# Order of the accumulating transfers of a head, and which weight loads the block copies follow, in a one-core hybrid block

## The chip, the core and the metric

The kernel runs on one core of one Trainium2 chip. The metric is the device time of one execution in microseconds (us); the time before is the median of three runs. A part of the reference's work is done on TensorE (called PE in the profile), with VectorE (DVE) and ScalarE (ACT) beside it; GpSimd (POOL) and SyncE (SP) issue the transfers, which sixteen DMA engines carry out.

## The reference

For 512 tokens of 1024 features the reference computes one layer: a projection with a wide weight matrix `w_in`, two mixers (a gated delta rule A with 8 heads, and a chunked retention B with 4 heads), their gated sum, and a feed-forward block. What the change touches is the part of `w_in` that makes the values and the gates of the four heads of mixer B:

```python
proj = xn @ w_in
qa, ka, va, za, beta_logit, a_dt, qb, kb, vb, gb, gate_a, gate_b = _split_cols(proj, IN_SIZES)
...
ob = chunk_retention(qb, kb, vb)
ob = rmsnorm(ob, norm_b.reshape(B_HEADS, B_DV)) * jax.nn.silu(gb.reshape(b, s, B_HEADS, B_DV))
yb = ob.reshape(b, s, B_V) @ w_br_b
```

For each head, `vb` and `gb` are 512 columns each.

## The kernel before, in words

**Products.** Every float32 product is made of three matmuls (`mm3`, L82 to L84) on a value that is split in a high and a low part. A weight is fetched 512 KB at a time by `weights` (L86): SP issues the load into one of the `raw` buffers (two in the first pool; a second pool adds two from head 0 of mixer B on), ACT casts it to its high part `whi` (L109), DVE subtracts to get the low part `wlo` (L110). `whi` and `wlo` have three buffers each. In most stages one such load feeds 24 matmuls of 128x512. Products land in four PSUM buffers `mm`, which ACT or DVE empty (for instance `acc`, L441 on ACT in the first partial product of a branch, L443 on DVE in the later ones). Engines run their instructions strictly in the order in which a scheduler wrote them at build time, so an ACT cast that waits for its load also holds up whatever ACT has behind it, and a DVE subtraction whatever DVE has behind it.

**Block sums.** The values and the gates of a head of mixer B are one product of four blocks by seven multiplications instead of eight (`values_and_gates`, L761). Four sums of weight blocks are needed for it; `BlockSums` (L116) makes them in DRAM without any compute engine. Each of the four sums `t[0]` to `t[3]` of a head has 1 MB and is handled in two halves of 512 KB (`k` is 0 or 2):

- A *copy* (L128) brings a first block from `w_in` to `t[i]`, DRAM to DRAM, on SP's queue. There are 32 of them. A list, `trickle`, holds them in the order head 0, 1, 2, 3; `weights` counts its loads from 0 (the counter `loads`) and issues one copy behind each load whose number is odd and at least 13 (L96 to L99).
- An *add* (`add`, L130) is an accumulating transfer that POOL issues: `t[2] += w12`, `t[1] += t[2]`, `t[3] += t[1]`, `t[0] += w12`, each in two halves. An add that reads another's result waits for it to land; POOL stands still while it waits. The eight adds of a head are issued behind one marked POOL instruction: head 0 and head 1 in stage A, behind the last transfer of `double_blocks` or the mask of `values_queries` (L719 to L721), heads 2 and 3 in mixer B behind the load of a decay table (L845 to L848).

The sums of head h are read back as weights (`raw<-sums`, L144) only when head h of mixer B is computed, from 592 us on for head 0.

**Stages.** Mixer A (up to about 540 us) has keys, values and queries, an inverse on DVE (L510 to L519) with small transfers on POOL's queue, four steps of a recurrence, gates, and the partial products of branch A (`ya_partial`, L436); then the four heads of mixer B, the output product, and the feed-forward block. The scheduler interleaves neighbouring stages.

**Order of work.** SP's queue carries loads and copies in one order; POOL's queue carries the adds, small memsets for the convolution (L397) and the small transfers of the inverse.

Of the kernel before, what the change touches and what calls it, by code (L numbers as in the profile page):

```python
# [15 lines left out]
ALU = mybir.AluOpType  # L16
# [44 lines left out]
def hybrid_block_kernel(ctx: ExitStack, tc: tile.TileContext, a: dict, out: bass.AP):  # L61
    nc = tc.nc
# [9 lines left out]
    trickle = []  # L72
# [13 lines left out]
    def weights(src, k0, nk, c0, ncols, keep=None):  # L86

        n = nk * ncols
        i = next(loads)
        pool, tag = raw_pools[i % len(raw_pools)]  # L90
        raw = pool.tile([P, 1024], F32, tag=tag, name="raw", bufs=2)
        load = nc.sync.dma_start(
            raw[:, :n].rearrange("p (k c) -> p k c", k=nk),
            src[k0 * P : (k0 + nk) * P, c0 : c0 + ncols].rearrange("(k p) c -> p k c", p=P),
        )
        if i >= 13 and i % 2 and trickle:  # L96
            sums, part, k = trickle.pop(0)
            with tc.issue_after(load.ins):
                sums.copy(part, k)  # L99
        return split_weights(raw, n, nk, keep, 200 if i >= 6 else 0)  # L100

    def split_weights(raw, n, nk, keep=None, ahead=200):
        if keep is None:
            hi = ring.tile([P, 1024], F32R, tag="whi", name="whi")
            lo = ring.tile([P, 1024], F32R, tag="wlo", name="wlo")
        else:
            hi, lo = keep
        with tc.high_priority(ahead):
            nc.scalar.copy(hi[:, :n], raw[:, :n])  # L109
            nc.vector.tensor_tensor(lo[:, :n], raw[:, :n], hi[:, :n], ALU.subtract)  # L110
        return (
            hi[:, :n].rearrange("p (k c) -> p k c", k=nk),
            lo[:, :n].rearrange("p (k c) -> p k c", k=nk),
        )

    class BlockSums:  # L116
# [12 lines left out]

        def add(self):  # L130

            for i in (2, 1, 3, 0):
                src = (self.w12, self.t[2], self.w12, self.t[1])[i]
                for k in range(0, 4, 2):
                    nc.gpsimd.dma_start(self.t[i][:, k : k + 2, :], src[:, k : k + 2, :], accum_op=ALU.add)

        def weights(self, i, ks):
            return block_weights(self.t[i - 1][:, 2 * ks : 2 * ks + 2, :])
# [8 lines left out]
    def feature_major(src, xs, c0, ncols, kts, krow0=0):  # L147

        nf = ncols // P
        pss = [psm.tile([P, xs[0].shape[2]], F32, tag="mm", name="mm") for _ in range(nf)]  # L150
        step = 1024 // ncols
        for k0 in range(0, kts, step):
            wh, wl = weights(src, krow0 + k0, step, c0, ncols)
            for f in range(nf):
                fs = slice(f * P, (f + 1) * P)
                for kk in range(step):
                    kt = k0 + kk
                    mm3(
                        pss[f],
                        (wh[:, kk, fs], wl[:, kk, fs]),  # L160
                        (xs[0][:, kt, :], xs[1][:, kt, :]),
                        kt == 0,
                        kt == kts - 1,
                    )
        return pss

    def token_major(src, lhs, c0, kts, krow0=0):

        pss = [psm.tile([P, T], F32, tag="mm", name="mm") for _ in range(4)]
        for k0 in range(0, kts, 2):  # L170
            wh, wl = weights(src, krow0 + k0, 2, c0, 512)
            for t in range(4):
                tt = slice(t * P, (t + 1) * P)
                for kk in range(2):
                    kt = k0 + kk
                    mm3(
                        pss[t],
                        [x[:, tt] for x in lhs(kt)],
                        (wh[:, kk, :], wl[:, kk, :]),
                        kt == 0,  # L180
                        kt == kts - 1,
                    )
        return pss
# [71 lines left out]
    with tc.tile_pool(name="xp", bufs=2) as xp:  # L255
# [30 lines left out]
        for pair in range(2):  # L286
            v = xp.tile([P, 2], F32, tag="xv", name="xv")
            for i in range(2):
                junk = xp.tile([P, D], BF16, tag="junk", name="junk")
                nc.scalar.activation(junk, xts[2 * pair + i], AF.Square, accum_out=v[:, i : i + 1])  # L290
            nc.vector.tensor_scalar(v, v, 1.0 / D, EPS, ALU.mult, ALU.add)
            y = root(v)
            rx += [y[:, i : i + 1] for i in range(2)]
            if pair == 0:
                wh, wl = weights(w_in, 0, 8, OFF_BA, P)
# [862 lines left out]
```

## Time and profile before

| | us |
|---|---|
| median of 3 runs | 1410.09 |
| lowest and highest | 1409.16, 1411.61 |
| the profiled execution, its own time | 1413.15 |
| its span, first to last instruction | 1411.4 |
| PE busy | 1378.8 |
| DVE busy | 868.5 |
| ACT busy | 613.5 |

The mean granted clock of TensorE was 0.991. In the profile a row of a timeline gives start, duration, engine, source line, what is written and read, and in brackets how long the engine had been idle and what ended the wait. A `q` behind an engine's name means its queue: an issue of a transfer, not work.

### The profile page before, as it was taken

What the parts mean: (1) busy time and instruction counts of PE and PEld (TensorE: products, weight loads), DVE (VectorE), ACT (ScalarE), POOL (GpSimd) and SP (SyncE); (2) the same over time, 40 slices, a digit from 0 to 9 for tenths busy, and PEclk for the clock granted to TensorE, in tenths of its full rate; (3) what the DMA queues carried; (4) which work ended last, traced back from release to release, by engine and by line L of the source; (5) the groups of instructions that cost most, each with busy time, mean ns of one, the idle gap of its engine ahead of it and who ended that gap; (6) DMA issues with size and microseconds to landing.
All of it is one profiled execution on the core that took longest, in us unless ns stands there. A gap on an engine that the chain in (4) does not pass through costs nothing.

```text
span 1411.4 us, 17607 instructions
## 1 busy us (share of the span) xinstructions
PE 1378.8 (98%) x6670; PEld 1128.3 (80%) x6670; DVE 868.5 (62%) x1539; ACT 613.5 (43%) x1134; POOL 87.7 (6%) x136
## 2 busy tenths in 40 slices
PE   8999999999999998999999999999999999999997
PEld 6888787877877877887878888878788888888886
DVE  5599889943755576367477577575685324344445
ACT  6777564724533332253453343443354333132331
POOL 1111300220020002000200000000000000000000
PEclk9999999999999999999999999999999999999999
DMA  5243513393384358663772442541714232323321
GB/s 157 75 122 105 152 56 105 101 185 117 113 187 133 124 178 186 192 201 102 175 229 67 140 136 89 187 143 61 251 65 146 90 104 90 105 90 104 105 75 60
DMA packets 88312, 180.08 MB, mean 128 GB/s; under 512 B 6080, under 2 KB 19538, under 8 KB 87715
## 3 DMA queue, kind: packets, MB, share of 16 engines
q1 hardware_dynamic: 77264, 148.39, 32.9%
q0 software_dynamic: 10240, 29.32, 9.8%
q8 instruction: 52, 0.85, 0.2%
q10 hardware_dynamic: 722, 1.25, 0.2%
q14 instruction: 34, 0.27, 0.1%
HBM read 173.17 MB, written 39.32 MB: 151 GB/s over the span
## 4 chain that ended last, share of the span: by engine, by line
PE 57%; DVE 3%; DMA 1%; ACT 1%; issue 1%; DVEq 0%; ACTq 0%; SPq 0%
PE mm L82 14%; PE mm L84 14%; PE mm L83 14%; PE mm L772 9%; PE dl L772 2%; PE dl L82 1%; PE dl L84 1%; PE dl L83 1%; PE tr L219 1%; DMA raw<-in_w_out_dram 1%; DVE wlo L110 0%; ACT whi L109 0%; DVE tb L966 0%; DVE actT L968 0%; DVE tb L965 0%
## 5 line engine op out<-in xcount | busy, mean ns | idle before, releaser
L110 DVE TENSOR_TENSOR wlo<-raw,whi 128x1024 fp32r<-128x1024 f32 x232 | 283.7, 1224 | 362.0 <-ACT whi L109 361.0
L109 ACT CAST whi<-raw 128x1024 fp32r<-128x1024 f32 x232 | 244.0, 1053 | 477.7 <-PE mm L83 228.7
L83 PE MATMUL mm<-actT,whi 128*128 128x512 f32 (+1 forms) x528 | 208.4, 395 | 1.0 <-DVE actT L253 1.0
L84 PE MATMUL mm<-actT,wlo 128*128 128x512 f32 (+1 forms) x528 | 208.3, 395 | 0.0
L82 PE MATMUL mm<-actT,whi 128*128 128x512 f32 (+1 forms) x528 | 207.0, 393 | 0.6 <-ACT actT L252 0.6
L82 PEld LDWEIGHTS mm<-actT,whi 128*128 128x128 f32 x528 | 100.1, 190 | 20.8 <-ACT actT L252 1.0
L83 PEld LDWEIGHTS mm<-actT,whi 128*128 128x128 f32 x528 | 100.3, 190 | 20.3 <-DVE actT L253 1.3
L84 PEld LDWEIGHTS mm<-actT,wlo 128*128 128x128 f32 x528 | 100.6, 190 | 18.7
L82 PE MATMUL mm<-og,whi 128*128 128x512 f32 x256 | 102.9, 402 | 11.9 <-DVE acc L443 8.6
L82 PE MATMUL mm<-hn,whi 128*128 128x512 f32 (+1 forms) x288 | 105.6, 367 | 0.5 <-DVE r L1081 0.5
L83 PE MATMUL mm<-hn,whi 128*128 128x512 f32 (+1 forms) x288 | 105.3, 366 | 0.0
L84 PE MATMUL mm<-hn,wlo 128*128 128x512 f32 (+1 forms) x288 | 105.1, 366 | 0.0
L83 PE MATMUL mm<-og,whi 128*128 128x512 f32 x256 | 102.2, 399 | 0.0
L84 PE MATMUL mm<-og,wlo 128*128 128x512 f32 x256 | 102.1, 399 | 0.0
L82 PE MATMUL mm<-whi,actT 128*128 128x512 f32 x216 | 86.2, 399 | 0.1
L83 PE MATMUL mm<-wlo,actT 128*128 128x512 f32 x216 | 85.7, 397 | 0.0
L84 PE MATMUL mm<-whi,actT 128*128 128x512 f32 x216 | 85.5, 397 | 0.0
L772 PE MATMUL mm<-whi,xsum 128*128 128x512 f32 x256 | 80.4, 390 | 1.6 <-ACT p L814 1.6
L407 DVE SCALAR_TENSOR_TENSOR c_y<-c_raw,convw,c_y 128x512 f32<-128x512 f32 x96 | 70.6, 752 | 3.3 <-ACT c_y L405 2.8
L82 PEld LDWEIGHTS mm<-og,whi 128*128 128x128 f32 x256 | 49.7, 194 | 24.1 <-DVE acc L443 4.8
L82 PEld LDWEIGHTS mm<-hn,whi 128*128 128x128 f32 x288 | 54.3, 189 | 10.1 <-DVE r L1081 0.8
L84 PEld LDWEIGHTS mm<-hn,wlo 128*128 128x128 f32 x288 | 54.2, 189 | 8.8
(319 smaller groups left out, 2472.8 us busy)
## 6 DMA issues: line engine op xcount, KB each, us to landing
raw<-in_w_in_dram SPq DMA_DIRECT2D x105, 512.0 KB, 3.7
raw<-in_w_up_dram SPq DMA_DIRECT2D x36, 512.0 KB, 3.6
sums<-in_w_in_dram SPq DMA_DIRECT2D x32, 512.0 KB, 5.0
raw<-sums SPq DMA_DIRECT2D x32, 512.0 KB, 4.3
raw<-in_w_down_dram SPq DMA_DIRECT2D x32, 512.0 KB, 3.6
raw<-in_w_br_a_dram SPq DMA_DIRECT2D x16, 512.0 KB, 3.8
sums<-in_w_in_dram POOLq DMA_DIRECT2D x16, 512.0 KB, 12.2
sums<-sums POOLq DMA_DIRECT2D x16, 512.0 KB, 12.1
```

The costliest lines, as they stand in the source:

```text
L82: nc.tensor.matmul(ps, lh, rh, start=first, stop=False)
L83: nc.tensor.matmul(ps, lh, rl, start=False, stop=False)
L84: nc.tensor.matmul(ps, ll, rh, start=False, stop=last)
L109: nc.scalar.copy(hi[:, :n], raw[:, :n])
L110: nc.vector.tensor_tensor(lo[:, :n], raw[:, :n], hi[:, :n], ALU.subtract)
L219: nc.tensor.transpose(ps, src, ident)
L407: nc.vector.scalar_tensor_tensor(y, raw[:, j : j + T], tap(j), y, ALU.mult, ALU.add)
L772: m = nc.tensor.matmul(pss[t], lhs[i // 2], rhs[i % 2], start=first and k + i == 0, stop=k + i == 5, skip_group_check=not first,)
```

## The change

Two edits. In `weights` the condition on odd numbers goes, so that each load from number 13 to number 44 is followed by a copy, instead of every second one from 13 to 75. In `add` the eight accumulating transfers are written in another order, by halves and so that each of the first six is followed by the one that depends on it, and they are pinned to that order (the scheduler may not rearrange them among each other).

```diff
-        if i >= 13 and i % 2 and trickle:
+        if i >= 13 and trickle:
             sums, part, k = trickle.pop(0)
             with tc.issue_after(load.ins):
                 sums.copy(part, k)
...
         def add(self):
 
-            for i in (2, 1, 3, 0):
+            for i, k in ((2, 0), (1, 0), (3, 0), (2, 2), (1, 2), (3, 2), (0, 0), (0, 2)):
                 src = (self.w12, self.t[2], self.w12, self.t[1])[i]
-                for k in range(0, 4, 2):
-                    nc.gpsimd.dma_start(self.t[i][:, k : k + 2, :], src[:, k : k + 2, :], accum_op=ALU.add)
+                add = nc.gpsimd.dma_start(self.t[i][:, k : k + 2, :], src[:, k : k + 2, :], accum_op=ALU.add)
+                tc.keep_in_program_order(add)
```

The adds of head 0 on POOL's queue, before (`sums_341` to `sums_344` are `t[0]` to `t[3]` of head 0):

```order
L135 DMA sums_343<-in_w_in_dram 128x2x512 x2
L135 DMA sums_341<-in_w_in_dram 128x2x512
L135 DMA sums_342<-sums_343 128x1024 x2
L135 DMA sums_341<-in_w_in_dram 128x2x512
L135 DMA sums_344<-sums_342 128x1024 x2
```

The same piece of POOL's queue now:

```order
L134 DMA sums_343<-in_w_in_dram 128x2x512
L134 DMA sums_342<-sums_343 128x1024
L134 DMA sums_344<-sums_342 128x1024
L134 DMA sums_343<-in_w_in_dram 128x2x512
L134 DMA sums_342<-sums_343 128x1024
L134 DMA sums_344<-sums_342 128x1024
L134 DMA sums_341<-in_w_in_dram 128x2x512 x2
```

Before, the three adds that depend on nothing stood first and could all be under way together. Now the second add needs the first and the third the second; the fourth needs none of those ahead of it, so it goes out right behind the third; the last two need none either and go out right behind the sixth. The other heads have the same order.

SP's queue where the adds of head 0 run (`br_a` is the weight of branch A; `sums<-in_w_in_dram` on SP is a copy), before:

```order
L92 DMA raw<-in_w_br_a_dram 128x2x512
L128 DMA sums<-in_w_in_dram 128x2x512
L92 DMA raw<-in_w_br_a_dram 128x2x512 x2
L128 DMA sums<-in_w_in_dram 128x2x512
L92 DMA raw<-in_w_br_a_dram 128x2x512
L92 DMA raw<-in_w_in_dram 128x2x512
L128 DMA sums<-in_w_in_dram 128x2x512
L92 DMA raw<-in_w_in_dram 128x2x512 x2
```

The same loads now:

```order
L92 DMA raw<-in_w_br_a_dram 128x2x512
L128 DMA sums<-in_w_in_dram 128x2x512
L92 DMA raw<-in_w_br_a_dram 128x2x512
L128 DMA sums<-in_w_in_dram 128x2x512
L92 DMA raw<-in_w_br_a_dram 128x2x512
L128 DMA sums<-in_w_in_dram 128x2x512
L92 DMA raw<-in_w_br_a_dram 128x2x512
L128 DMA sums<-in_w_in_dram 128x2x512
L92 DMA raw<-in_w_in_dram 128x2x512
L128 DMA sums<-in_w_in_dram 128x2x512
```

Each load there has a copy behind it now, where every second one had. Where the adds of head 1 run, at the next partial product of branch A, the queue was this before:

```order
L92 DMA raw<-in_w_br_a_dram 128x2x512
L128 DMA sums<-in_w_in_dram 128x2x512
L92 DMA raw<-in_w_br_a_dram 128x2x512 x2
L128 DMA sums<-in_w_in_dram 128x2x512
L92 DMA raw<-in_w_br_a_dram 128x2x512
L92 DMA raw<-in_w_in_dram 128x2x512
L128 DMA sums<-in_w_in_dram 128x2x512
L92 DMA raw<-in_w_in_dram 128x2x512 x2
```

Now, from the last copy of all (its row is the first here) to the queries of mixer B:

```order
L128 DMA sums<-in_w_in_dram 128x2x512
L92 DMA raw<-in_w_in_dram 128x2x512 x4
L92 DMA raw<-in_w_br_a_dram 128x2x512 x4
L92 DMA raw<-in_w_in_dram 128x2x512 x4
L92 DMA raw<-in_w_br_a_dram 128x2x512 x4
L92 DMA raw<-in_w_in_dram 128x4x256 x4
```

No copy is left beside the adds of heads 1, 2 and 3. On PE, ACT and DVE the scheduler also rearranges neighbouring instructions between the second and the third step of the recurrence (some 195 to 292 us of the trace); behind that their order is as before.

## The prediction

> **What bounds the kernel now.** I read the page first, then who PE waits for.
>
> ```profile
> span 1411.4 us, 17607 instructions
> PE 1378.8 (98%) x6670; PEld 1128.3 (80%) x6670; DVE 868.5 (62%) x1539; ACT 613.5 (43%) x1134; POOL 87.7 (6%) x136
> ```
>
> ```profile
> PE mm L82 <- DVE acc L443: 8.6, 2, 4.4
> PE mm L82 <- ACT acc L441: 3.1, 1, 3.1
> ```
>
> PE is busy for 98% of the span, and the change takes no matmul away. What can be won is idle time of PE, 32.6 us in all, and time in which its clock is throttled. The three longest waits of the program stand in these two rows (columns: total us, times, longest); a fourth of 1.59 us follows below. PE's timeline tells where they are; I show the last matmuls ahead of the first one, to read their spacing, and then the matmul behind each wait:
>
> ```profile
> 319.22 0.39 PE L83 MATMUL mm<-og,whi 128*128 128x512 f32 x1
> 319.45 0.39 PE L84 MATMUL mm<-og,wlo 128*128 128x512 f32 x1
> 322.89 0.50 PE L82 MATMUL mm<-og,whi 128*128 128x512 f32 x1 [3.05 <-ACT acc L441]
> ...
> 424.91 0.76 PE L82 MATMUL mm<-og,whi 128*128 128x512 f32 x1 [4.18 <-DVE acc L443]
> ...
> 543.84 0.80 PE L82 MATMUL mm<-og,whi 128*128 128x512 f32 x1 [4.43 <-DVE acc L443]
> ...
> 719.50 0.50 PE L772 MATMUL mm<-whi,xsum 128*128 128x512 f32 x1 [1.59 <-ACT p L814]
> ```
>
> Each lies where a head's adds run. Of those I show POOL's rows for the first three adds of head 0 and the fourth issue of head 1, which is the first to wait for another add's landing:
>
> ```profile
> 287.12 3.59 POOL L135 DMA_DIRECT2D sums<-in_w_in_dram  x3
> ...
> 404.60 0.86 POOL L135 DMA_DIRECT2D sums<-sums  x1 [3.73 <-DMA sums<-in_w_in_dram]
> ```
>
> The windows view gives what a wait costs behind it (columns: stretch, length, busy time and count of PE, PEld, DVE, ACT, POOL, then granted clock, DMA share, GB/s):
>
> ```profile
> 287.00:325.00 38.00, 34.95 (x238) 27.83 (x237) 15.86 (x25) 9.49 (x13) 8.22 (x9) 0.99 0.96 195
> 322.90:328.00 5.10, 5.10 (x15) 4.05 (x16) 0.87 (x2) 1.24 (x2) 0.00 (x0) 0.67 0.76 253
> 423.00:430.00 7.00, 5.09 (x12) 4.05 (x13) 4.78 (x6) 1.05 (x1) 0.00 (x0) 0.51 1.04 270
> 542.50:549.30 6.80, 5.46 (x13) 4.30 (x14) 3.08 (x5) 0.00 (x0) 0.86 (x1) 0.50 1.07 198
> ```
>
> Behind the first wait the clock loses 0.33 x 5.1 = 1.7 us, behind the second 0.49 x 7.0 = 3.4 us, behind the third as much. So the first episode (head 0) costs 3.05 + 1.7 = 4.8 us, the second (head 1) 4.18 + 3.4 = 7.6 us, the third (head 2) 4.43 + 3.4 = 7.8 us, and the fourth (head 3) 1.59 us.
>
> Next, why ACT and DVE were late. ACT at the first, DVE at the second and the third:
>
> ```profile
> 321.31 1.04 ACT L109 CAST whi<-raw 128x1024 fp32r<-128x1024 f32 x1 [5.11 <-DMA raw<-in_w_in_dram]
> 322.26 0.58 ACT L441 COPY acc<-mm 128x512 f32<-128x512 f32 x1
> ```
>
> ```profile
> 422.94 1.23 DVE L110 TENSOR_TENSOR wlo<-raw,whi 128x1024 fp32r<-128x1024 f32 x1 [8.47 <-ACT whi L109]
> 424.08 2.47 DVE L443 TENSOR_TENSOR acc<-acc,mm 128x512 f32<-128x512 f32 x4
> ...
> 541.97 1.22 DVE L758 TENSOR_TENSOR xsum<-full,xsum 128x1024 fp32r<-128x1024 f32 x1
> 543.10 2.48 DVE L443 TENSOR_TENSOR acc<-acc,mm 128x512 f32<-128x512 f32 x4
> ```
>
> In the first two, the copy that frees PE's PSUM buffer stands behind a split of a weight that has not landed: DMA is the cause. In the third DVE has no idle time at all: it computes the sums of the features (L758) ahead of `acc`, so no transfer can shorten it. Here are the two late loads, with SP's issues:
>
> ```profile
> 307.47 0.37 SPq L92 DMA_DIRECT2D raw<-in_w_in_dram  x1
> ...
> 401.68 0.65 SPq L128 DMA_DIRECT2D sums<-in_w_in_dram  x1
> 406.70 0.37 SPq L92 DMA_DIRECT2D raw<-in_w_br_a_dram  x1
> ```
>
> The first took from 307.47 until the cast at 321.31 was released, some 13.8 us; the second from 406.70 to about 421.8 (422.94 on DVE less a cast of 1.05), 15.1 us. A quiet stretch (340 to 375 us) and then head 0's adds (287 to 325 us), from the DMA view (share of 16 engines; us to landing):
>
> ```profile
> q1 hardware_dynamic: 1377, 2.16, 19.9%
> raw<-in_w_in_dram SPq DMA_DIRECT2D x4, 512.0 KB, 3.5
> ...
> q0 software_dynamic: 1733, 4.26, 68.3%
> q1 hardware_dynamic: 1614, 3.12, 27.4%
> ```
>
> SP's transfers (q1) take 0.199 x 35 us / (2.16 MB / 0.524 MB) = 1.7 us of all engines each. The eight adds (q0) take 0.683 x 38 us / 8 = 3.24 us each. While adds are queued they hold two thirds of the engines without a pause, and a load needs 9 to 15 us where a quiet one needs 3.5. PE eats a load in 24 x 0.227 us = 5.44 us (spacing of the rows above).
>
> **The change part by part.** *One add at a time.* The price of a lone add is not in the trace; nearest are the first add of head 1 and, for a load that has only adds beside it, the one issued at 682.02 us in head 3:
>
> ```profile
> sums<-in_w_in_dram POOLq DMA_DIRECT2D x1, 512.0 KB, 7.0
> ...
> raw<-in_w_in_dram SPq DMA_DIRECT2D x1, 512.0 KB, 9.4
> ```
>
> A head's chain is then 7.0 (first), 7.0 (second), 7.0 + 3.24 (third and fourth go out together), 7.0 (fifth), 7.0 + 2 x 3.24 (the last three together): 45 us, of which the engines hold adds for 8 x 3.24 = 26 us. Before, the same 26 us were packed in 38. Nobody waits for the end of it: head 0's sums are read from 592 us on, and POOL's next work behind head 0 is a memset that comes at 374 us here:
>
> ```profile
> 374.15 0.10 POOL L397 MEMSET c_raw<- 128x3 f32 x1 [61.46 <-DVE c_y L411]
> ```
>
> Seven more us of chain are hidden in its wait of 61 us; without that cover they would be PE time.
>
> *Head 1.* No copy is left on SP's queue. PE stopped at 424.91 - 4.18 = 420.7; cast, split and `acc` need 1.05 + 1.23 + 0.8 us ahead of that, so the load of 406.70 may land as late as 417.5: 10.8 us after its issue. With one add in flight (the second one, which can start when the first has landed, at 404.6, and takes to about 411.6) it takes 3.5 us plus at most 3.24: it lands by 413.5. The next loads meet two adds at most: 3.5 + 2 x 3.24 = 10.0, still under 10.8. Gain 7.6; lower bound of the gain 3.4 (if a shorter wait stays that spares only the clock), and I take 7.6.
>
> *Head 0.* Here copies are denser, one behind each load, so SP needs 2 x 1.7 us in 5.44 us, 63% of the engines, where it had 47%. PE stopped at 319.8; a cast of 1.04 and `acc` of 0.58 must be done by then, so the load of 307.47 may land until 318.2 (10.7 us). At that time the third and fourth add are under way with about 3.4 us left, and one copy stands ahead on SP's queue: 3.5 + 3.4 + 1.7 = 8.6 us, on time by 2 us. The next one has one add and one copy ahead: 8.4 us, on time. The load behind it goes out at about 318 and, two loads of 5.44 us later by the same reckoning, must land by 329; the last three adds begin at 287.1 + 31 = 318. It takes between 3.5 + 1.7 + 3.24 = 8.4 and 15.1, the landing of the load of 406.70 with a copy ahead. That is the weak spot. I take it as 1 us late, without a throttled clock: gain 4.8 - 1.0 = 3.8. Bounds: a gain of 4.8, or a new wait of 4 us with 3.4 of clock, a loss of 2.6.
>
> *Head 2.* The wait of 4.43 us is DVE's, no transfer ends it, and no other wait of PE of over 0.5 us lies in the stretch of these adds: 0, and at most 0.3 either way. *Head 3.* No copies before or after; the adds' hold is looser now but its product uses up a load in 12 x 0.227 = 2.7 us, so it stays the tightest of the four: gain between 0 and 1.59, I take 0.8.
>
> *Copies earlier.* Between 83 and 290 us twice as many copies run. A copy can hold the next load by 1.7 us; the casts of that stretch wait for PE and never for a transfer. So 0 as long as loads stay ahead of PE as they do there; without that cover each late load would cost up to 1.7 us. *The rearranged piece*:
>
> ```profile
> 195.00:292.00 97.00, 96.72 (x655) 77.79 (x652) 84.66 (x223) 53.22 (x139) 18.04 (x28) 1.00 0.35 102
> ```
>
> PE idles for 0.28 us in 97, with DVE 87% busy: another order there can hardly win and may lose. I take 0.5 us of loss for both, from 0 to 3 (as long as the first of the four waits).
>
> **Sum**: -7.6 - 3.8 - 0.8 + 0.5 = -11.7 us. On the profiled execution's span that is 1411.4 - 11.7 = 1399.7; its own time was 1413.15, 3.1 us above the median of the runs. I carry the difference over to the median: 1410.1 - 11.7 = 1398.4 us.
>
> **The rivals.** *Head 0 keeps its wait.* The last three adds and the dense copies meet, or a load pays a fixed number of turns however many adds are queued. For it: the load of 682.02 took 5.9 us more than a quiet one, 1.8 adds. Against it: a single add in flight has only 3.24 us to give. Then head 1 still gains (9.4 is under 10.8), head 0 nothing: 1410.1 - 7.6 - 0.8 + 0.5 = 1402.2. The Trainium skill, page "DMA: Bandwidth & Descriptors", section on queues, rings and completion order, has such a rule: an engine takes turns between queues and empties a whole packet of some 9 to 17 descriptors from one before it goes to the next, so what waits behind the first add would not count. The trace agrees only in part: by one turn the load would have been 3.24 us late, and it was 5.9.
>
> *No change.* Adds hold up loads by their sum, wherever they stand, and head 1's wait only moves to the burst at the chain's end. Against it: a load must take 10.8 us to stop PE there, and one or two adds give at most 10.0. Time: 1410 within 2 us.
>
> *Slower, in head 0.* The engines stay as full as now through the longer chain: SP gets 27.4% of 45 us, 7.25 transfers, and half of them are copies, so 3.6 loads arrive where PE wants 45 / 5.44 = 8.3. Now 4.1 arrive of 7, a shortage of 2.9 that costs 3.05 us. A shortage of 4.7 is 1.8 x 5.44 = 9.8 us more idle time, and 1.7 more of clock: 11.5. With the other terms: -7.6 - 0.8 + 0.5 + 11.5 = +3.6, 1413.7 us. It decides if adds hold the engines for more than the 26 of 45 us that I count, so that their share there is near 68% again. Against it: the third add cannot start before the second has landed, and in those pauses SP has the engines alone.
>
> **How the numbers follow.** The forecast has 0.47 (1394.5 to 1400.5), head 0 keeping its wait 0.28, no change 0.08, slower 0.10; 0.05 for a rearranged piece that costs 3 us or more (1401 to 1407), 0.02 for a larger gain. The range from 1394 to 1407 holds the first, the second and the fifth, 0.80. Its lower end is a gain of 13.9 (4.8 + 7.6 + 1.59) and 2 us for the spread of the runs; its upper end is the second case with 3 us for the rearranged piece and 1.8 for the spread. A measurement of this kernel can tell about 0.2%, 2.8 us, from no change: faster by more 0.82, within it 0.08, slower by more 0.10.
>
> **What would show it.** Right: no wait of PE near 425 us and a clock of 1.00 there, the wait at 543 still of 4.4 us but some 11 us earlier; loads beside head 1's adds landing in 4 to 8 us; DMA share in head 1's 45 us near 0.85 rather than 1.04. Wrong: ACT still waiting for `raw` for over 5 us beside head 1's adds, PE waits of over 1 us between 80 and 290 us, or a wait of PE of 4 us and a throttled clock some 10 us later than the one at 322.9.

## The result, and the profile after

The changed kernel takes 1402.58 us, the median of six runs, against 1410.36 us for the kernel before, also of six: a ratio of 0.9944 with a 95% interval from 0.9930 to 0.9957, so 7.8 us or 0.56% less. (One of the six, 1885.53 us at a granted clock of 0.681, was a disturbed run and is left out of the ratio; without it the median is 1402.02 us.) The forecast was 1398.4 us in a range of 1394 to 1407. The profiled execution took 1403.7 us, its span was 1402.0 us, 9.4 us shorter than the span before.

The head of the page:

```profile
span 1402.0 us, 17608 instructions
PE 1373.8 (98%) x6670; PEld 1125.1 (80%) x6670; DVE 869.2 (62%) x1539; ACT 613.4 (44%) x1134; POOL 86.4 (6%) x136
```

PE's busy time fell by 5.0 us although it does the same 6670 matmuls: that is mainly clock, whose mean rose from 0.991 to 0.994 (0.9% of 1411 us lost before, 0.6% of 1402 now). Next, PE's waits by who ended them (total us, times, longest):

```profile
PE mm L82 <- DVE acc L443: 4.4, 1, 4.4
PE dl L82 <- ACT osq L904: 2.2, 1, 2.2
...
PE dl L650 <- ACT vn L645: 1.6, 2, 0.8
```

The row `mm <- DVE acc` has lost one of its two waits, `mm <- ACT acc` is gone from this view, and a new row stands second. PE's timeline tells where each lies:

```profile
263.15 1.13 PE L650 MATMUL dl<-vn,kd 128*128 128x256 f32 x4 [0.81 <-ACT vn L645]
...
330.86 0.70 PE L650 MATMUL dl<-vn,kd 128*128 128x256 f32 x2 [0.81 <-ACT vn L645]
...
533.80 0.79 PE L82 MATMUL mm<-og,whi 128*128 128x512 f32 x1 [4.40 <-DVE acc L443]
...
725.91 0.50 PE L82 MATMUL dl<-vr,s 128*128 128x512 f32 x1 [0.69 <-DVE p L824]
...
733.16 0.50 PE L82 MATMUL dl<-vr,s 128*128 128x512 f32 x1 [2.20 <-ACT osq L904]
```

The waits of 3.05 us (head 0) and 4.18 us (head 1) are gone, that of head 2 is the same, 10 us earlier, and head 3's single wait of 1.59 us has become two, 2.9 us together. The windows give the clock (columns as in the prediction; the column to read is the eighth, after POOL): the stretches of the adds of heads 0 and 1, then what follows the waits of heads 2 and 3:

```profile
287.80:342.60 54.80, 53.99 (x333) 43.43 (x332) 25.48 (x40) 21.11 (x38) 8.14 (x9) 1.00 0.93 212
394.20:444.50 50.30, 50.30 (x231) 41.10 (x231) 29.82 (x54) 17.41 (x32) 8.08 (x9) 1.00 0.84 167
...
532.50:539.70 7.20, 5.90 (x14) 4.64 (x15) 3.04 (x5) 0.00 (x0) 0.86 (x1) 0.53 0.80 172
733.10:738.10 5.00, 4.94 (x15) 3.89 (x16) 1.32 (x3) 1.39 (x5) 0.00 (x0) 0.66 0.07 24
```

Heads 0 and 1 now run at full clock. Head 3 does not: behind its wait at 733 us the clock loses 0.34 x 5.0 = 1.7 us. Head 3 cost 1.59 us before and costs 0.69 + 2.20 + 1.7 = 4.6 us now. Why there? POOL's queue at head 3:

```profile
670.22 1.23 POOL L134 DMA_DIRECT2D sums<-in_w_in_dram  x1
...
695.85 0.85 POOL L134 DMA_DIRECT2D sums<-sums  x1 [10.11 <-DMA sums<-in_w_in_dram]
706.22 0.81 POOL L134 DMA_DIRECT2D sums<-sums  x1 [9.52 <-DMA sums<-sums]
706.75 2.63 POOL L134 DMA_DIRECT2D sums<-in_w_in_dram  x2
```

The last three adds of the eight go out together, 36 us after the first (the row of 706.75 holds two), and SP issues six loads just then:

```profile
705.47 16.21 SPq L92 DMA_DIRECT2D raw<-in_w_in_dram  x6
```

This is the dense stage of the head, whose product uses up a load in 2.7 us. The next view is ACT behind it:

```profile
718.98 1.05 ACT L109 CAST whi<-raw 128x1024 fp32r<-128x1024 f32 x1 [4.22 <-DMA raw<-in_w_in_dram]
...
722.96 1.05 ACT L109 CAST whi<-raw 128x1024 fp32r<-128x1024 f32 x1 [1.88 <-DMA raw<-in_w_in_dram]
...
732.42 0.60 ACT L904 ACTIVATE osq<-dl 128x512 f32<-128x512 f32 x1
```

Two casts wait for their loads (issued at 708.66 and 710.91 us and landed 10.2 and 11.9 us later), DVE and ACT carry the delay on, and ACT empties a PSUM buffer (`osq`) at 732.4, for which PE waits. That this chain begins with the three adds is so far an inference from neighbouring rows; the experiments test it.

### The profile page after: what moved, and what is told of

Its sections match the earlier page's. It is cut to its first block, busy times and chain, and to the rows that moved or that the text cites. A ratio compares the mean times of both kernels' runs of the same rounds, so it can differ in the third digit from the quotient of the medians.

```text
span 1402.0 us, 17608 instructions
## 1 busy us (share of the span) xinstructions
PE 1373.8 (98%) x6670; PEld 1125.1 (80%) x6670; DVE 869.2 (62%) x1539; ACT 613.4 (44%) x1134; POOL 86.4 (6%) x136
## 3 DMA queue, kind: packets, MB, share of 16 engines
q0 software_dynamic: 10240, 29.32, 10.5%
## 4 chain that ended last, share of the span: by engine, by line
PE 55%; DVE 3%; DMA 2%; ACT 1%; issue 1%; DVEq 0%; ACTq 0%; SPq 0%
PE mm L82 14%; PE mm L84 14%; PE mm L83 14%; PE mm L772 9%; PE dl L772 1%; PE dl L82 1%; PE dl L84 1%; PE dl L83 1%; DMA raw<-in_w_in_dram 1%; PE tr L219 1%; DMA raw<-in_w_out_dram 1%; DVE wlo L110 1%; ACT whi L109 0%; DVE tb L966 0%; DVE actT L968 0%
## 5 line engine op out<-in xcount | busy, mean ns | idle before, releaser
L82 PE MATMUL mm<-og,whi 128*128 128x512 f32 x256 | 101.1, 395 | 4.6 <-DVE acc L443 4.4
L83 PE MATMUL mm<-og,whi 128*128 128x512 f32 x256 | 100.7, 393 | 0.0
L82 PEld LDWEIGHTS mm<-hn,whi 128*128 128x128 f32 x288 | 54.3, 188 | 10.2 <-DVE r L1081 0.8
L83 PEld LDWEIGHTS mm<-hn,whi 128*128 128x128 f32 x288 | 54.3, 188 | 8.6
```

What stands on the lines that cost most here:

```text
L82: nc.tensor.matmul(ps, lh, rh, start=first, stop=False)
L83: nc.tensor.matmul(ps, lh, rl, start=False, stop=False)
```

## The experiments

The theory stated after the result, "adds in flight": how late a load lands depends on how many adds are under way beside it, so one add at a time costs PE nothing, and what the forecast missed is head 3's three together. Rivals: the copies did it; total demand (each add costs its share of the engines wherever it stands); the dependent order itself; adds that cost time without a visible wait. All times below are medians beside runs of the kernel before on the same chip, whose medians were 1409.14, 1409.29 and 1409.22 us in the three groups.

### The two edits apart

Only the first edit, in the kernel before:

```diff
-        if i >= 13 and i % 2 and trickle:
+        if i >= 13 and trickle:
```

> Only the first edit: a copy behind each load from the 14th to the 45th; the adds stand in the old order, the three that depend on nothing together at the front. Theory of adds in flight (a load beside several adds lands late, and one add at a time leaves it room): head 0 now has bunched adds and twice the copies beside its loads, so its wait of 3.05 us stays or grows (3 to 7 us, with the half clock behind it 5 to 10 us lost, where the changed kernel loses 0.8); head 1 has bunched adds without copies, its latest load 15.0 us under way before less two copies of 1.7 us = 11.6 us against the 10.8 us allowed, so a wait of about 1 us in place of 4.18; head 3 as before, 1.59 us. Sum 1410.4 - 6.6 + 2 = about 1406 us (1403 to 1411). Rival, the copies alone did it (the copies beside head 1's adds made the long landing and the new order does nothing): head 1 at no wait, head 0 as before, 1410.4 - 7.6 = 1402.8 us.

Measured: 1410.97 us, ratio 1.0012 (0.9999 to 1.0025): nothing, or a small loss. PE's timeline, and the window behind the first wait:

```profile
326.82 0.79 PE L82 MATMUL mm<-og,whi 128*128 128x512 f32 x1 [5.25 <-ACT acc L441]
...
426.40 0.47 PE L82 MATMUL mm<-og,whi 128*128 128x512 f32 x1 [0.60 <-DVE acc L443]
...
442.85 0.33 PE L219 MATMUL tr<-cmat,vt 128*128 128x128 f32 x1 [1.71 <-DVE og L203]
...
530.02 0.49 PE L82 MATMUL mm<-og,whi 128*128 128x512 f32 x1 [1.21 <-DVE ro L836]
```

```profile
326.10:333.00 6.90, 6.18 (x15) 4.84 (x16) 2.45 (x2) 2.30 (x4) 0.00 (x0) 0.51 0.61 180
```

Head 1's wait shrinks from 4.18 to 0.60 us, head 0's grows from 3.05 to 5.25, and the half clock behind it costs 3.0 us instead of 1.7 (0.49 of the 6.18 us in which PE was busy). By these rows the kernel would still win 2.6 us (5.25 + 3.0 + 0.60 = 8.9 where the two episodes cost 4.8 and 6.7 by the same count); two waits that the kernel before does not have, the last two rows, take 2.9 back. The first of them stands behind a load issued at 425.69 us that took 10.5 us; what makes the second stays open. The time is at the upper end of what was expected (1403 to 1411).

Only the second edit, in the changed kernel with the old condition:

```diff
-        if i >= 13 and trickle:
+        if i >= 13 and i % 2 and trickle:
```

> Only the second edit: the adds in the new pinned order; the copies stay behind every second load, so that head 1's adds again have copies beside them. Theory of adds in flight: head 0's wait of 3.05 us and head 1's of 4.18 us both go (at most two adds under way until the end of each head), head 3 has the same three adds together at its end and the same new waits of 0.69 and 2.20 us: 1402.6 us as the changed kernel (1400.5 to 1405). Rival, the copies did it: head 1's wait of 4.18 us stays with the half clock behind it, 1402.6 + 7.6 = 1410 us, or in part, 1406.

Measured: 1402.10 us, ratio 0.9944 (0.9924 to 0.9965), the whole effect of the change. The waits of the two heads are absent though copies again stand beside head 1's adds, and head 3's new one is there (the first row is a wait at 11.3 us, far ahead of all adds):

```profile
PE tr L219 <- DVE xn L300: 4.5, 1, 4.5
PE mm L82 <- DVE acc L443: 4.4, 1, 4.4
PE dl L82 <- ACT osq L904: 2.2, 1, 2.2
```

PE's order is that of the kernel before from end to end in this run, so the rearranged piece, which comes with the copies' condition, is not the gain either. So the order of the adds is the change. The copies' new place brings nothing that can be told beside it, and by itself moves waiting from head 1 to head 0.

### Head 3's three adds

One add at a time, in the changed kernel. A small transfer reads what an add wrote, and POOL waits for it:

```diff
+            self.seen = {i: dr.tile([1, 4, 8], F32, tag=f"{tag}seen{i}", name="seen", bufs=1) for i in (0, 3)}
...
                 tc.keep_in_program_order(add)
+                if (i, k) in ((3, 0), (3, 2), (0, 0)):
+                    seen = nc.gpsimd.dma_start(self.seen[i][:, k : k + 1, :], self.t[i][:1, k : k + 1, :8])
+                    tc.keep_in_program_order(seen)
```

> The changed kernel, and a small transfer behind the third, sixth and seventh add of a head that reads what the add wrote, so that POOL waits there for its landing and no two adds are ever under way together. The order on PE, ACT, DVE and SP is that of the changed kernel. A head's adds take 8 x 7 us and some 6 us for the three small transfers, 62 us in place of 50 to 55. Theory of adds in flight: the loads of head 3 that were issued at 708.66, 710.91 and 716.25 and took 10.2, 11.9 and 9.6 us beside the last three adds land within 8 us, the waits of 0.69 and 2.20 us at 726 and 733 us and the half clock of 3.4 us behind them go: 1402.6 - 4.6 = 1398.0 us (1396.5 to 1399.5). Rival, total demand: the stage from 700 to 727 us loads 512 KB every 2.7 us, and any add in it, one by one or together, costs the same 3.24 us of all engines; now three adds still lie in it, the landings stay at 10 us and the waits at 2 to 3 us: 1402 to 1403 us.

Measured: 1396.58 us (1396.08 to 1396.96), ratio 0.9908 (0.9890 to 0.9925). POOL's queue at the end of head 3, ACT's casts of the same stage, and PE's longest waits:

```profile
709.69 0.81 POOL L135 DMA_DIRECT2D sums<-sums  x1 [9.27 <-DMA sums<-sums]
716.82 0.54 POOL L138 DMA_DIRECT2D seen<-sums  x1 [6.32 <-DMA sums<-sums]
717.34 1.23 POOL L135 DMA_DIRECT2D sums<-in_w_in_dram  x1
727.01 0.54 POOL L138 DMA_DIRECT2D seen<-sums  x1 [8.44 <-DMA sums<-in_w_in_dram]
727.53 1.20 POOL L135 DMA_DIRECT2D sums<-in_w_in_dram  x1
```

```profile
709.69 1.05 ACT L109 CAST whi<-raw 128x1024 fp32r<-128x1024 f32 x1 [1.37 <-DMA raw<-sums]
...
717.71 1.05 ACT L109 CAST whi<-raw 128x1024 fp32r<-128x1024 f32 x1 [0.31 <-PE dl L776]
720.43 1.05 ACT L109 CAST whi<-raw 128x1024 fp32r<-128x1024 f32 x1 [1.67 <-PE mm L776]
```

```profile
PE mm L82 <- DVE acc L447: 4.4, 1, 4.4
PE tr L223 <- DVE o L914: 1.6, 4, 0.4
```

Adds still run through the dense stage, until 735 us, but singly, and the casts that waited for loads there now wait for PE. Is the demand the same? For the same stretch of PE's work (687.3 to 739.5 us in the changed kernel, 686.0 to 733.0 here) the DMA view gives the adds 34.4% of 52.2 us there and 39.5% of 47.0 here: 18.0 and 18.6 us of all engines. Total demand over the stage is refuted: as much of it costs PE nothing here. In the densest 25 us alone it is less, 8.5 us against 11.1, so over so short a piece demand and number in flight are not fully told apart. Nor are all landings short: the load issued at 717.9 us, right behind a single add, took 9.3 us, and PE had the slack for it. By its median this is the fastest version.

The second way is to take the adds out of that stage, with no other edit to the changed kernel:

```diff
-            if h in (1, 2):
+            if h in (0, 1):
                 with tc.issue_after(decay.ins):
-                    vg_sums[h + 1].add()
+                    vg_sums[h + 2].add()
```

> The changed kernel with the adds of head 2 issued behind the decay table of head 0 of mixer B (in place of head 1's), and those of head 3 behind that of head 1 (in place of head 2's). So no add lies in the stage at 670 to 727 us whose loads follow each other every 2.7 us; head 2's adds move to some 460 to 520 us. Theories of adds in flight and of total demand alike: the waits of 0.69 and 2.20 us at 726 and 733 us and the half clock behind them go, 1402.6 - 4.6 = 1398.0 us, if head 2's adds wake no new wait where they now lie (0 to 3 us: no row shows them there): 1397 to 1401. Rival, those waits are not due to the loads but to ACT's and DVE's own work in head 3: they stay, 1402.6 us.

Measured: 1398.58 us, ratio 0.9921 (0.9903 to 0.9939), as expected, and no wait at 726 or 733 us.

Then the small transfers for some heads only. For head 3 alone:

```diff
-                if (i, k) in ((3, 0), (3, 2), (0, 0)):
+                if self is vg_sums[3] and (i, k) in ((3, 0), (3, 2), (0, 0)):
```

> The changed kernel, with the small reading transfers behind head 3's adds alone; heads 0 to 2 end with three adds together as in the changed kernel. Theory: the missing 4 us of the prediction lie in head 3's last three adds. Then its waits at 726 and 733 us and the half clock behind them (4.6 us) go, heads 0 to 2 stay as they are: 1402.6 - 4.6 = 1398.0 us (1396.5 to 1399.3). Rival, the gain of one add at a time (6 us) is spread over the heads: 1399.5 to 1401.5 us.

For heads 0 to 2, with `self is not vg_sums[3]` in the same line:

> The counterpart: the small reading transfers behind the adds of heads 0, 1 and 2, and head 3 as in the changed kernel, with its last three adds together. Theory: head 3 keeps its waits of 0.7 and 2.2 us and the half clock: 1396.6 + 4.6 = 1401.2 us (1400 to 1402.8). Rival, the gain is spread over the heads: 1398.5 to 1400 us.

Measured: head 3 alone 1397.80 us (1397.59 to 1398.13), ratio 0.9918 (0.9905 to 0.9930); heads 0 to 2 1403.22 us (1400.02 to 1406.80), ratio 0.9957 (0.9941 to 0.9973). PE's second row of waits in each, head 3 alone first:

```profile
PE dl L654 <- ACT vn L649: 2.4, 2, 1.5
```

```profile
PE dl L82 <- DVE p L828: 3.6, 1, 3.6
```

With head 3 alone 1402.6 - 1397.8 = 4.8 us go, where 4.6 were reckoned from the trace; as the kernel before took 1410.36 us beside the one and 1409.22 beside the other, the ratios to it are the safer measure (0.9918 against 0.9944), and by them 3.7 go. Without head 3 nothing goes, and a wait of 3.6 us stands in head 3. The second median lies 0.4 us above the range given for it; its runs spread over 7 us, so the 0.6 us by which it is above the changed kernel say nothing.

### Order, copies, or number in flight

The old order by sums, `((2, 0), (2, 2), (1, 0), (1, 2), (3, 0), (3, 2), (0, 0), (0, 2))`, with the small transfer behind each add but the last:

```diff
-                if (i, k) in ((3, 0), (3, 2), (0, 0)):
+                if (i, k) != (0, 2):
```

> The adds in the order of the kernel before (by sums, t[2], t[1], t[3], t[0], both halves of each), but with a small transfer behind each of the first seven that reads what it wrote, so that POOL waits for its landing: never two adds under way, and no chain of dependent adds in the order. Copies as in the changed kernel. Theory of adds in flight: only how many are under way at a time counts, the dependent order is one means to that; so no wait at 720 to 735 us, none at head 0 and head 1, and the time of the run with one add at a time in the new order, 1396.6 us (1395.8 to 1397.6). Rival, the dependent order itself does good (an add that reads what has just been written is cheaper, or the halves matter): some of the waits of head 0 or head 3 come back, 1399 to 1404 us.

The new order one at a time, with the old condition on the copies (the edit of the adds alone, above):

> One add at a time in the new order (the small reading transfers), and the copies behind every second load as in the kernel before. Theory of adds in flight: with one add at a time the copies beside head 1's adds cost nothing, as they did not beside the changed order: 1396.6 us (1395.5 to 1398.5). Rival, the copies beside the adds still cost something there: a wait of 1 to 4 us at head 1, 1398 to 1404 us.

No add at all:

```diff
-            for i, k in ((2, 0), (1, 0), (3, 0), (2, 2), (1, 2), (3, 2), (0, 0), (0, 2)):
+            for i, k in ():
```

> The changed kernel without any add: the sums of blocks hold only what the copies brought, so a part of the values and gates of mixer B is left out of the computation. PE, ACT and DVE run the same instructions. It says what all 32 adds still cost. Theory of adds in flight: in the run with one add at a time no wait of PE stood in the adds' stretches, so nothing is left to win: 1396.3 us (1395 to 1397). Rival, the adds also cost time that shows as no wait (slower work on the engines while they run): 2 us or more less, 1392 to 1394.5 us.

Measured: old order 1397.88 us, ratio 0.9921 (0.9901 to 0.9940); copies behind every second load 1397.22 us, 0.9914 (0.9896 to 0.9931); no add 1397.70 us, 0.9910 (0.9892 to 0.9928). With one add at a time (1396.58 us, 0.9908) these are four kernels with overlapping intervals: the order, the copies and the adds themselves cost nothing that can be told once no two adds are under way together (each interval is some 2.5 us wide to either side). The old order and the run without adds lie 0.3 and 0.7 us above the ranges given for them, whose point values were 1396.6 and 1396.3. PE's first row of waits without adds:

```profile
PE mm L82 <- DVE acc L443: 4.4, 1, 4.4
```

Head 2's wait is there without any add, so no order of adds could have taken it away.

Last, the mirror of the changed order, three together in front and single ones at the end:

```diff
-            for i, k in ((2, 0), (1, 0), (3, 0), (2, 2), (1, 2), (3, 2), (0, 0), (0, 2)):
+            for i, k in ((2, 0), (0, 0), (1, 0), (0, 2), (3, 0), (2, 2), (1, 2), (3, 2)):
```

> The changed kernel with the two halves of t[0] moved from the end of a head's adds to the front: t[2] first half, t[0] first, t[1] first, t[0] second, t[3] first, then t[2], t[1], t[3] second. So two or three adds are under way together at the front and single ones at the end, the mirror of the changed order; a head's adds take some 45 us. Theory of adds in flight: head 3's three together now lie at 670 to 690 us, where the loads follow each other every 5.4 us and have 7 to 20 us to spare, and single adds beside the loads of the dense stage: its waits of 0.69 and 2.20 us shrink to 0 to 1.6 us; head 0 and head 1 have three together at 288 to 310 and 394 to 412 us, where no load was late in the changed kernel, 0 to 2 us. Together 1399 us (1396.5 to 1402). Rival, total demand in a head's stretch: the same eight adds in 45 us instead of 50 to 55 cost as in the kernel before, waits of 3 to 4 us at head 0 or 1 come back, 1405 to 1410 us.

Measured: 1404.97 us, ratio 0.9967 (0.9955 to 0.9979). The expectation of 1399 failed by 6 us. PE's timeline and the window behind its second wait:

```profile
321.96 0.50 PE L82 MATMUL mm<-og,whi 128*128 128x512 f32 x1 [1.67 <-ACT acc L441]
...
333.74 0.85 PE L650 MATMUL dl<-vn,kd 128*128 128x256 f32 x2 [2.22 <-ACT vn L645]
...
736.49 0.50 PE L82 MATMUL dl<-vr,s 128*128 128x512 f32 x1 [0.65 <-ACT osq L904]
```

```profile
334.20:337.70 3.50, 3.50 (x13) 3.01 (x12) 1.35 (x2) 0.69 (x1) 0.00 (x0) 0.52 0.99 214
```

Head 3 is nearly clear, as reckoned. Head 0 pays 1.67 + 2.22 + 0.48 x 3.5 = 5.6 us: its third group of adds goes out at 306.3 and 306.85 us with one more still under way, and the load issued at 307.92 beside it took 12.35 us. Head 1 pays another 1.24 us at 437.3 us, behind a load issued at 419.92 that took 10.7. The total-demand rival named 1405 us by waits of 3 to 4 us at head 0 or 1, which is about what stands there; this run does not refute it. One add at a time refutes it in head 3 only: at head 0 the eight adds then take 67 us (287.5 to 354.7) where they take 55 in the changed kernel, so there number in flight and demand per time fall together, and no run separates them. Nor do three adds together always do harm. The last three of head 1 in the changed kernel made a load take 11.3 us (issued at 430.56), and PE did not wait; what decides is whether the load beside them has time to spare.

How a load's landing grows with adds under way, from the traces of eleven kernels (the kernel before, the changed one and all above but the one without adds): 512 KB loads issued in and near the heads' stretches, taken by the number of adds under way at their issue (an add whose landing was not recorded is not counted), and only those with little other traffic (less than half another load or copy beside them on average):

| adds under way | loads | median landing, us | lowest to highest |
|---|---|---|---|
| 0 | 161 | 3.7 | 3.5 to 5.7 |
| 1 | 107 | 5.1 | 3.6 to 9.5 |
| 2 | 11 | 8.6 | 6.9 to 10.1 |
| 3 | 13 | 10.1 | 8.1 to 12.6 |

The Trainium skill's page "DMA: Bandwidth & Descriptors" (section on queues, rings and completion order) says that an engine goes round its queues packet by packet; by that rule as the prediction read it, what waits behind the first add would not count. The table differs from this reading: from one add to two the median rises by 3.5 us, about the 3.24 us of engine time that the prediction took for an add, and a third adds 1.5. But the reading took a whole add for one turn, and the DMA views in the prediction count 1733 packets for eight adds, 217 each, and 270 to 330 for a load. Taking turns by packet, a load beside queued adds would meet up to as many of their packets as it has itself, 270 to 330 times 3.24 / 217 us, 4 to 5 us (an estimate). So a second add would count and a third hardly; the 4.9 us above a quiet load for two adds agree, the 6.4 for three, on 13 loads, lie above.

## Why the prediction was right, and where it was off

Its sign and its main mechanism held; its size was 4 us too good. PE runs the same matmuls in the same order behind the rearranged piece, so the start of one matmul in both traces tells what the kernel has won up to there:

| a matmul | before, us | now, us | difference |
|---|---|---|---|
| ahead of head 0's wait | 299.95 | 300.89 | +0.9 |
| between heads 0 and 1 | 380.20 | 377.10 | -3.1 |
| between heads 1 and 2 | 504.88 | 494.90 | -10.0 |
| between heads 2 and 3 | 639.66 | 629.80 | -9.9 |
| behind head 3 | 779.78 | 773.15 | -6.6 |
| ahead of the output product | 1004.69 | 998.16 | -6.5 |

By the prediction's own steps:

| step | forecast, us | measured, us |
|---|---|---|
| head 1 | -7.6 | -6.9 |
| head 0 | -3.8 | -4.0 |
| head 2 | 0 | +0.1 |
| head 3 | -0.8 | +3.2 |
| earlier copies, rearranged piece | +0.5 | +0.9 |
| sum | -11.7 | -6.6 |

The medians differ by 1410.36 - 1402.58 = 7.8 us (6.1 to 9.9 by the interval of the ratio), the spans by 9.4. What the spans have beyond the 6.6 lies outside the change. The kernel before had two waits and a half clock at the output product, a stage of its own far behind the last add:

```profile
1018.35 0.50 PE L82 MATMUL mm<-keep,actT 128*128 128x512 f32 x1 [0.90 <-ACT keep L109]
1019.61 0.50 PE L83 MATMUL mm<-keep,actT 128*128 128x512 f32 x1 [0.76 <-DVE keep L110]
```

```profile
1020.30:1023.80 3.50, 3.50 (x10) 2.71 (x9) 0.00 (x0) 0.00 (x0) 0.00 (x0) 0.51 0.89 326
```

The changed kernel had one of 0.76 us there and no half clock: 0.90 + 0.49 x 3.5 = 2.6 us in its favour. In other profiles the pair comes and goes (it is there in both kernels with one edit, and not with one add at a time). That fits the prediction's carrying of the profiled execution's 3.1 us of surplus over to the median: about as much belonged to that execution.

*Head 1* was right but for 0.7 us. The sum counted the clock's loss over the whole row of 423 to 430 us, 0.49 x 7.0; PE was busy for 5.09 us of it and stood in the wait, counted already, for the rest. 0.49 x 5.09 = 2.5 us and the wait of 4.18 make 6.7. (Head 2's 7.8 has the same slip, 0.50 x 5.46 in place of 3.4, without effect on the sum.) Its reason was half of the truth: the step named one add in flight and copies gone, and with the adds' order alone the wait is gone with the copies still there.

*Head 0*, "the weak spot", was right: the wait and its half clock went, and 0.8 us of it came back at 330.86 us, where 1.0 was forecast. As the step said, it takes the dense copies and the last three adds to make it: the wait is absent with the adds' order alone and with one add at a time. The rival that head 0 keeps its wait named 1402.2 us, which is nearer to the time measured than the forecast, and is wrong all the same: the wait is gone, and the missing 4 us lie elsewhere; that it came so near is luck. A time that agrees does not prove a mechanism. The slower rival's premise, adds on the engines for 68% of the chain, is refuted by the DMA view of head 0's stretch, which has 50%:

```profile
q0 software_dynamic: 1732, 4.26, 50.1%
```

The chain itself was longer than the 45 us reckoned: 54.8 us at head 0, 50.3 at head 1, 51.8 at head 3, and 45.2 only at head 2, where few transfers compete. As forecast, nobody waited for its end.

*Head 3* is the step that failed: "the adds' hold is looser now". It is looser on average, and the step was judged by the average. The same text had worked out that the last three adds of a chain go out together, and had looked at what they meet in head 0; it did not look at what they meet in head 3. Its chain put them 31 us behind the first, at 670 + 31 = 701 us, into loads every 2.7 us. The price was there too: three adds of 3.24 us on a load of 3.5 us make 13.2 us, where the loads took 10.2 and 11.9. The run with head 3 alone wins back most of the difference: 1397.8 us, or 3.7 us by the ratios. That this is 0.6 from the forecast is partly luck, as the forecast also had head 1 too large.

*Copies earlier and the rearranged piece* cost 0.9 us, mainly the wait at 263.15 us, within the 0 to 3 given. That wait comes and goes too: with PE's order as in the changed kernel it is absent without adds and with the small transfers at heads 0 to 2.

Not settled: why the half clock behind a wait of 2.2 us at 733 us comes in one run and not in another (below), which makes up to 1.7 us of the spread of the kernels with bunched adds; and whether at head 0 the number in flight or the adds' demand per time is what counts.

## What to carry to other kernels

Judge background transfers by how many are under way beside the tightest loads, not by their share of a long stretch: a chain that is thin on average still does harm where its free members bunch. A dependent order is only one way to thin them; a tiny transfer that reads the last result limited the queue to one here, in either order. When a reorder moves a burst, look up what stands at its new place in every repetition of the loop, since the stages differ.

## What the runs showed that was not expected

Small transfers that make POOL wait are cheap: 12 of them cost nothing that can be told (1396.58 us with them, 1397.70 us with no add at all).

Between the first 25 us and the last 10 the half clock came only in pieces of about 3.4 us or 6.8 us, and the wait ahead of it does not decide it alone. Head 2's wait of 4.2 to 4.4 us, in all twelve traces, was followed by 6.8 us of it in eight and by 3.4 in four. And 2.20 us at 733 us was followed by it in the changed kernel, while 2.19 us at the same instruction was not with the second edit alone:

```profile
732.04 0.50 PE L82 MATMUL dl<-vr,s 128*128 128x512 f32 x1 [2.19 <-ACT osq L904]
```

```profile
732.00:738.00 6.00, 5.96 (x26) 4.96 (x27) 2.86 (x11) 1.96 (x6) 0.00 (x0) 1.00 0.04 17
```

So a wait of some 2 us can cost its length or its length and 1.7 us, and a forecast should carry both.
